# A decoder trunk whose MLP's second matrix goes in seven half-block products, woven with the first matrix of the next rows, and sums of its weights made by accumulating DMAs in DRAM

## The chip, the cores and the metric

The kernel runs on one core of a Trainium2 chip. The metric is device time in microseconds (us), the median of several executions. The engines are named as the profile names them: PE (TensorE, matrix products), DVE (VectorE), ACT (ScalarE), POOL (GpSimd) and SP (SyncE, which here only issues DMAs). PEld is PE's loading of the stationary operand, which runs beside the products.

## The reference, cut to what matters

One sequence of 1024 tokens, width 1024, goes through two layers. Layer 0 mixes tokens with attention and a gated delta rule, layer 1 with a recurrent block. After each mixer comes a layer norm, then an MLP of hidden width 4096, then a second norm.

```python
def sqrelu_mlp(x, w1, w2):
    h = jax.nn.relu(x @ w1)          # (1024, 1024) @ (1024, 4096)
    return (h * h) @ w2              # (1024, 4096) @ (4096, 1024)

def reference(x, ...):
    for layer in range(DEPTH):       # DEPTH = 2
        ...
        x = layer_norm(DN_ALPHA * x + mix, ln1_g[layer], ln1_b[layer])
        x = layer_norm(DN_ALPHA * x + sqrelu_mlp(x, mlp_w1[layer], mlp_w2[layer]),
                       ln2_g[layer], ln2_b[layer])
    return x
```

All is float32 with an output of (1, 1024, 1024).

## The kernel before

**Products.** Each float32 operand is split into a rounded part h and a residue l. A product is then three matmuls, h by h, h by l and l by h (`mm3`, line 359), added up in one PSUM bank. One matmul has 128 x 128 stationary elements and up to 512 moving columns. In the tables a "product" of PE is one such matmul.

**Weights.** `wblock` (line 339) loads a block of 128 x 1024 elements (512 KB) on SP's queue into one of three buffers `ws`, and splits it by halves: the rounded copy `wh` on ACT (every fifth half on DVE), the residue `wl` by turns on POOL and DVE. There are four half-block buffers for each of `wh` and `wl`, thus two blocks.

**Two streams.** The tokens go in two chunks of 512 rows, stream 0 and stream 1 (`stream`, line 1158). Stream 1 needs stream 0's states in the mixers, so it runs behind it. All of PE's work is put into one fixed order at build time. The driver loop (line 1190) asks the streams' generators for work: a `yield UNIT` ends a piece after which another stream may come next, a `yield BLOCK` means that a stream waits for buffers or for the other. The stream with the lowest `phase` (0 for mixers, 1 and 2 for the two MLPs) comes first; recurrent blocks (`light`) take turns with the other stream. Small mixer parts and norms are spawned as generators of their own and come in when a rough model of the engines (class `Clock`) says that their operands are there. The other engines' order is made by the tile framework's scheduler, with a simulated timeline.

**Buffers.** `gpool` has 14 granules of 128 x 2048 elements (`g`): an activation matrix with its residue (`ActT`) takes four, the residual rows `yg` of a stream two. Rings `t` (11), `s` (9) and `f` (4) hold tiles of 128 x 516. PSUM has four banks `mm` and four `mx`.

**MLP** (`mlp`, line 500). Eight passes e, each over 512 hidden columns. First matrix: four blocks by `proj_fm` (line 412), each 24 matmuls into one bank; ACT applies Relu and Square, POOL squares again in full precision, DVE makes the residue; the results (`s`) are hidden columns on partitions. Second matrix: for each half of the 1024 outputs, two blocks, 48 matmuls into four banks, which DVE then adds to y (128 x 512 each). In the last pass DVE also makes the norm's statistics (`bn_stats`). The last pass of stream 1 in layer 1 goes row block by row block, so that the final norm can start early.

**Norms** (`layernorm`, line 450). DVE makes the coefficients, ACT, DVE and POOL scale the eight halves, PE transposes them, ACT and DVE split the transposed rows into h and l. `mix_out` (line 1117) does a mixer's output projection (`out_proj`) and then such a norm; `mlp_ln` (line 1131) does an MLP and the norm behind it.

**Recurrent block** (`rec_block`, line 944). Four for each stream, each with four projection blocks of 24 matmuls, one block of gate weights (24 matmuls), and a chain of about 20 operations on ACT and DVE for each of its two columns, in tiles of ring `t`.

## Time and profile before

| | us |
|---|---|
| median of 3 runs | 2389.71 |
| lowest, highest | 2389.05, 2390.38 |
| span of the profiled execution | 2384.5 |
| PE busy | 2298.9 |
| DVE busy | 1345.1 |
| ACT busy | 912.7 |
| POOL busy | 843.0 |

The span goes from the first to the last instruction; the profile gives no total time of its own execution, and the median lies 5.2 us above the span. Busy times of different engines overlap. A busy time in a matmul's or vector operation's row includes its pipeline, so operations that follow one another start closer together than their mean durations say. All compute operations that the planner's wrappers issue have line 177 or, for PE, 204 and 207; the tiles' names tell them apart: `wh`, `wl`, `ws` are weights, `g` granules, `mm` and `mx` PSUM, `w` in a DMA an MLP matrix, `hout` and `rout` output projections, `rin` and `rg` recurrent weights.

### The profile page before, as it was taken

To read this page: it belongs to the slowest core of one execution; us is meant where nothing else is said; L and a number is where in the kernel's file an instruction comes from. 1 tells how busy PE (TensorE), PEld (TensorE's weight loads), DVE (VectorE), ACT (ScalarE), POOL (GpSimd) and SP (SyncE) were. 2 spreads that over 40 slices of the span, in tenths; PEclk is the share of its full clock that TensorE was granted. 3 is DMA by queue.
4 is the path that set the end of the run, shared out by engine and by line. 5 is a ranking of instruction groups with operands and counts; after the bars stand their busy time and mean duration, and the time that the engine had idled before them with its cause. 6 is when DMAs were issued, how large, how long until landed. Compare 5 with 4: busy or idle time off the path is not lost. (4 is left out here: it accounts for less than half of the span.)

```text
span 2384.5 us, 33354 instructions
## 1 busy us (share of the span) xinstructions
PE 2298.9 (96%) x12724; PEld 1841.9 (77%) x12724; DVE 1345.1 (56%) x2550; ACT 912.7 (38%) x1813; POOL 843.0 (35%) x706
## 2 busy tenths in 40 slices
PE   8889997999999999999999999999999999999997
PEld 7666775677777878778887788877887788778876
DVE  7697659565754463755664623565665543633345
ACT  5364424443333242454443322344554232322331
POOL 3342334232332243433443432343333333433341
PEclk9999998999999999999999999999999999999999
DMA  4121231122233222322333222232325222332231
GB/s 154 54 81 31 81 124 36 54 69 74 73 114 110 95 88 98 123 89 97 98 131 125 82 96 97 97 121 91 98 93 177 85 97 97 107 115 98 98 117 51
DMA packets 67487, 227.43 MB, mean 95 GB/s; under 512 B 7424, under 2 KB 7808, under 8 KB 67328
## 3 DMA queue, kind: packets, MB, share of 16 engines
q1 hardware_dynamic: 58832, 204.01, 25.9%
q10 hardware_dynamic: 8496, 21.30, 2.5%
q8 instruction: 100, 1.64, 0.3%
q14 instruction: 59, 0.48, 0.1%
HBM read 216.89 MB, written 8.39 MB: 94 GB/s over the span
## 5 line engine op out<-in xcount | busy, mean ns | idle before, releaser
L177 POOL TENSOR_TENSOR wl<-ws,wh 128x512 fp32r<-128x512 f32 (+1 forms) x372 | 497.6, 1338 | 1261.4 <-ACT wh L177 979.4
L204 PE MATMUL mm<-g,wh 128*128 128x512 f32 x2816 | 886.7, 396 | 0.5 <-DVE g L177 0.5
L177 ACT CAST wh<-ws 128x512 fp32r<-128x512 f32 (+1 forms) x595 | 365.5, 616 | 993.0 <-PE mm L204 910.1
L204 PE MATMUL mm<-wh,s 128*128 128x512 f32 x1984 | 648.2, 399 | 11.4 <-ACT s L177 5.7
L204 PEld LDWEIGHTS mm<-g,wh 128*128 128x128 f32 x2816 | 520.2, 189 | 107.2 <-issue 2.9
L204 PE MATMUL mm<-g,wl 128*128 128x512 f32 x1408 | 550.9, 391 | 5.4 <-POOL wl L177 5.4
L204 PEld LDWEIGHTS mm<-wh,s 128*128 128x128 f32 x1984 | 374.0, 189 | 102.6 <-ACT s L177 6.2
L204 PE MATMUL mm<-wl,s 128*128 128x512 f32 x992 | 391.9, 395 | 2.3 <-POOL wl L177 1.4
L177 DVE TENSOR_TENSOR wl<-ws,wh 128x512 fp32r<-128x512 f32 (+1 forms) x372 | 281.2, 756 | 188.8 <-ACT wh L177 184.4
L204 PEld LDWEIGHTS mm<-g,wl 128*128 128x128 f32 x1408 | 265.1, 188 | 64.0 <-POOL wl L177 7.1
L204 PE MATMUL mm<-wh,g 128*128 128x512 f32 (+1 forms) x768 | 235.2, 380 | 10.0 <-ACT wh L177 6.1
L177 DVE TENSOR_TENSOR s<-s,s 128x512 fp32r<-128x512 f32 x128 | 100.4, 784 | 242.9 <-POOL s L177 231.1
L204 PEld LDWEIGHTS mm<-wl,s 128*128 128x128 f32 x992 | 187.4, 189 | 43.3 <-POOL wl L177 1.8
L177 DVE TENSOR_TENSOR g<-g,mm 128x512 f32<-128x512 f32 x224 | 144.0, 680 | 130.7 <-PE mm L204 130.5
L204 PEld LDWEIGHTS mm<-wh,g 128*128 128x128 f32 x768 | 142.0, 190 | 38.7 <-ACT wh L177 6.1
L177 DVE CAST wh<-ws 128x512 fp32r<-128x512 f32 (+1 forms) x149 | 73.8, 495 | 172.6 <-PE mm L204 165.0
L177 POOL TENSOR_TENSOR s<-s 128x512 f32<-128x512 f32 x128 | 145.3, 1135 | 26.4 <-ACT s L177 26.4
L204 PE MATMUL mm<-wl,g 128*128 128x512 f32 (+1 forms) x384 | 143.7, 374 | 0.1
L177 ACT ACTIVATE s<-mm 128x512 f32<-128x512 f32 x128 | 75.9, 593 | 62.1 <-PE mm L204 61.9
L177 ACT ACTIVATE s<-s 128x512 fp32r<-128x512 f32 (+1 forms) x136 | 83.5, 614 | 19.0 <-DVE s L177 8.0
L204 PEld LDWEIGHTS mm<-wl,g 128*128 128x128 f32 x384 | 72.9, 190 | 11.9 <-DVE wl L177 0.4
L204 PE MATMUL mx<-g,wh 128*128 128x512 f32 x256 | 78.8, 389 | 0.0
(209 smaller groups left out, 2230.3 us busy)
## 6 DMA issues: line engine op xcount, KB each, us to landing
ws<-w SPq DMA_DIRECT2D x256, 512.0 KB, 3.3
ws<-hin_fm SPq DMA_DIRECT2D x32, 512.0 KB, 3.3
ws<-rin SPq DMA_DIRECT2D x32, 512.0 KB, 3.3
ws<-hout SPq DMA_DIRECT2D x16, 512.0 KB, 3.4
ws<-rout SPq DMA_DIRECT2D x16, 512.0 KB, 3.4
t<-ln ACTq DMA_DIRECT2D x28, 256.0 KB, 4.2
ws<-hin_q SPq DMA_DIRECT2D x8, 512.0 KB, 3.2
g<-x ACTq DMA_DIRECT2D x8, 512.0 KB, 5.0
```

The source lines that it names most:

```text
L177: r = f(*a, **k)
L204: return self._pe(self.pe.matmul(out, lhsT, rhs, start=start, stop=stop), out, [lhsT, rhs], c, start)
```

## The change

**Seven products.** Where it applies, a quarter j of the hidden width (1024 columns, two passes) is treated as a 2 x 2 block product: the hidden activations of 512 rows as two row halves (256 rows) by two column halves (512), the second matrix's quarter as two by two blocks of 512 x 512. In place of eight block products there are seven (`seven`), on combinations of the blocks. The combinations of activations are made by four DVE operations in place, 1024 elements wide. The combinations of weights `t1` to `t4` are sums that are ready in DRAM. Three accumulators of two banks each are begun; later products add on to a bank that has already been read (`kept`, banks `mm` and `mx`), and what stands there after each product is added to, or subtracted from, y.

**Sums of weights.** `w2_sums` is spawned in stream 0's first mixer. For each layer and quarter it copies four blocks of 1 MB from DRAM to DRAM on SP's queue and adds seven more by accumulating DMAs on POOL's queue, in rounds. `seven` waits in the build order until a quarter's sums are issued; on the chip the loads wait for their data.

**The MLP's order.** `first` makes the hidden values of one quarter and stores them unsplit, without POOL. `weave` then alternates one first-matrix block of the next quarter with two units of `seven` of this one. The straight passes stay where the condition fails: stream 0 until stream 1's output projection of the layer is through, at even e and with two granules free. In stream 1 of layer 1 pass 6 goes straight first, and the last pass (`ends`, `finish`) keeps its order by rows; its four hidden tiles are stored unsplit and split by `finish` after the last weave.

**Waits between the streams.** Stream 1's norm behind a mixer waits (`hold`) until stream 0's MLP has used its last first-matrix block (`m7`); stream 0's norm behind MLP 0 waits for the same of stream 1. Stream 1's recurrent block b waits for stream 0's block b, and uses ring `s` in place of `t`.

**Weights.** Three buffers of whole blocks in place of four of half blocks, split by one operation 1024 wide for each part; in `first` and `seven` the residue is always DVE's. The second matrix is stored by quarters and blocks.

```diff
-WB, HV, LG = 4, 5, 2
-RINGS = dict(t=11, s=9, f=4)
+WB, WS, HV, LG = 3, 3, 5, 2
+RINGS = dict(t=11, s=10, f=4)
...
+    def split(h, l, x, key):
+        wcount[0] += 1
+        (V.tensor_copy if wcount[0] % HV == 0 else S.copy)(h, x)
+        (G if key else V).tensor_tensor(l, x, h, ALU.subtract)
+    def wblock(src, n=1024, hl=None, pool=True):
+        st = clk.tile("ws", WS, wpool.tile([P, 1024], F32, tag="ws", name=nm("ws"), bufs=WS))[:, :n]
+        DS.dma_start(st if len(src.shape) == 2 else st.rearrange("p (q c) -> p q c", q=2), src)
+        if hl is None:
+            hl = [clk.tile(t, WB, wpool.tile([P, 1024], F32R, tag=t, name=nm(t), bufs=WB))[:, :n] for t in ("wh", "wl")]
+        h, l = hl
+        split(h, l, st, pool and wcount[0] % LG)
...
-    def proj_fm(src, x, bank=None):
-        wh, wl = wblock(src)
+    def proj_fm(src, x, bank=None, pool=True):
+        wh, wl = wblock(src, pool=pool)
...
+    SUMS = dict(t1=("b11", "b12"), t3=("b12", "b22"), t2=("b11", "b12", "b22"), t4=("b11", "b12", "b22", "b21"))
+    QUARTER = dict(b11=0, b12=1, b22=2, b21=3)
+    tsum = [[{k: dpool.tile([2 * P, D], F32, name=f"{k}_{i}_{j}", tag=f"{k}_{i}_{j}") for k in SUMS} for j in range(4)]
+            for i in range(2)]
+    def w2_quarter(layer, j, q):
+        return tsum[layer][j][q] if q in SUMS else I[f"w2_{layer}"][j * 4 + QUARTER[q]]
+    summed = set()
+    kept = [0]
+    def w2_sums():
+        rows = lambda x: x.rearrange("(a b) c -> a (b c)", b=2)
+        for layer, j in ((i, j) for i in range(2) for j in range(4)):
+            for k, (first, *_) in SUMS.items():
+                DS.dma_start(rows(tsum[layer][j][k]), rows(w2_quarter(layer, j, first)))
+            for i in range(1, 4):
+                t = clk.now + 8.0
+                yield lambda: t
+                for k, v in SUMS.items():
+                    if i < len(v):
+                        DG.dma_start(rows(tsum[layer][j][k]), rows(w2_quarter(layer, j, v[i])), accum_op=ALU.add, max_dma_last_dim=2048)
+            summed.add((layer, j))
+            t = clk.now + 8.0
+            yield lambda: t
...
+    def mlp(layer, c, yT, yg, ls, res=None):
+        w1 = I[f"w1_{layer}"]
+        seen = set()
+        def accumulate(ps, n, half, sign, done):
+            y = ytile(yg, n)[:, half * 512:(half + 1) * 512]
+            op = ALU.add if sign > 0 else ALU.subtract
+            if (n, half) not in seen:
+                seen.add((n, half))
+                V.scalar_tensor_tensor(y, y, ALPHA, ps, ALU.mult, op)
+            else:
+                V.tensor_tensor(y, y, ps, op)
+            if done:
+                V.bn_stats(ls[:, n, 6 * half:6 * half + 6], y)
+        either = lambda n: next((r for r in "st" if rings[r] >= n), None)
+        left = [32]
+        def used():
+            left[0] -= 1
+            if left[0] == 0:
+                yT.free()
+                st[c]["m7"] = layer
+        def straight(e, done):
+            j, i = divmod(e, 2)
+            yield from wait(lambda: either(8))
+            ring = either(8)
+            own = [(ts(ring, F32R), ts(ring, F32R)) for _ in range(4)]
             for f in range(4):
+                h, l = own[f]
                 ps = yield from proj_fm(w1[e * 4 + f], yT)
-                h, l, r = ts("s", F32R), ts("s", F32R), ts("s")
+                used()
+                r = clk.tile("r", 2, wpool.tile([P, 512], F32, tag="r", name=nm("r"), bufs=2))
                 S.activation(r, ps, AF.Relu)
                 S.activation(h, r, AF.Square)
                 G.tensor_tensor(r, r, r, ALU.mult)
                 V.tensor_tensor(l, r, h, ALU.subtract)
-                free("s", r)
-                sh.append(h)
-                sl.append(l)
-                if e == 7 and f == 3:
-                    yT.free()
                 yield UNIT
-            if e == 7 and res is not None:
-                for n in range(NT):
-                    a, b = n * P, (n + 1) * P
-                    for half in range(2):
-                        ps = mm_ps()
-                        for f in range(4):
-                            wh, wl = wb[half * 2 + f // 2]
-                            mm3(ps, sh[f][:, a:b], sl[f][:, a:b], wh[f % 2], wl[f % 2], f == 0, f == 3)
-                            yield
-                        y = ytile(yg, n)[:, half * 512:(half + 1) * 512]
-                        V.tensor_tensor(y, y, ps, ALU.add)
-                        V.bn_stats(ls[:, n, 6 * half:6 * half + 6], y)
-                    res["n"] = n + 1
-                    if n == 0:
-                        res["start"]()
-                    yield UNIT
-                free("g", *own)
-                free("s", *sh, *sl)
-                return
...
+        def hidden(f, z):
+            ps = yield from proj_fm(w1[f], yT, mm_ps, False)
+            used()
+            S.activation(z, ps, AF.Relu)
+            S.activation(z, z, AF.Square)
+            yield UNIT
+        def seven(j, g, done):
+            yield from wait(lambda: (layer, j) in summed)
+            A = {f"a{r + 1}{q + 1}": v4(g[q])[:, :, r * 256:(r + 1) * 256] for q in range(2) for r in range(2)}
+            bank = {}
+            for i, (a, b, acc, out, sign, last) in enumerate((
+                    ("a12", "b21", "R", (0, 0), 1, False), ("a11", "b11", "X", (0, 0), 1, True),
+                    ("a21", "t1", "R", (1, 1), 1, False), ("a21", "t2", "X", (0, 1), -1, False),
+                    ("a12", "b22", "R", (0, 1), 1, True), ("a21", "t3", "X", (1, 1), -1, True),
+                    ("a22", "t4", "X", (1, 0), 1, True))):
+                if i == 2:
+                    V.tensor_tensor(A["a21"], A["a21"], A["a22"], ALU.subtract)
+                elif i == 3:
+                    V.tensor_tensor(A["a21"], A["a21"], A["a11"], ALU.subtract)
+                elif i == 4:
+                    V.tensor_tensor(A["a12"], A["a12"], A["a21"], ALU.add)
+                elif i == 5:
+                    V.scalar_tensor_tensor(A["a21"], A["a21"], -1.0, A["a22"], ALU.mult, ALU.subtract)
+                start = i < 3
+                if start:
+                    bank[acc] = [(mm_ps if acc == "X" else mx_ps)() for _ in range(2)]
+                    kept[0] += 2 * (acc == "X")
+                for p in range(2):
+                    yield from wait(lambda: either(2))
+                    ring = either(2)
+                    ah, al = ts(ring, F32R), ts(ring, F32R)
+                    ah2, al2 = (z.rearrange("p (k t) -> p k t", k=2) for z in (ah, al))
+                    x = A[a][:, 2 * p:2 * p + 2]
+                    S.copy(ah2, x)
+                    V.tensor_tensor(al2, x, ah2, ALU.subtract)
+                    wh, wl = wblock(w2_quarter(layer, j, b)[p * P:(p + 1) * P], pool=False)
+                    for k in range(2):
+                        for t in range(2):
+                            mm3(bank[acc][t], ah2[:, k, t * P:(t + 1) * P], al2[:, k, t * P:(t + 1) * P], wh[k], wl[k],
+                                start and p + k == 0, p + k == 2, not start)
+                            if p + k == 2:
+                                accumulate(bank[acc][t], 2 * out[0] + t, out[1], sign, done and last)
+                            if k + t < 2:
+                                yield
+                    free(ring, ah, al)
+                    if i == 6 and p == 1:
+                        free("g", *g)
+                        kept[0] -= 2
+                    yield UNIT
+        def first(j):
+            yield from need("g", 2)
+            g = [gran() for _ in range(2)]
+            for f in range(8):
+                yield from hidden(j * 8 + f, v4(g[f // 4])[:, f % 4, :])
+            hids[j] = g
+        def weave(a, b, every):
+            left = [(a, 1), (b, every)] if a is not None else [(b, every)]
+            while left:
+                stuck = True
+                for gen, k in list(left):
+                    for _ in range(k):
+                        r = next(gen, "end")
+                        if r is BLOCK:
+                            break
+                        stuck = False
+                        while r is not UNIT and r != "end":
+                            yield r
+                            r = next(gen, "end")
+                        if r == "end":
+                            left.remove((gen, k))
+                            break
+                        yield UNIT
+                if stuck:
+                    yield BLOCK
+        hids = {}
+        e = 0
+        if res is not None:
+            yield from straight(6, False)
+        while e < 8 and not ((c == 1 or sts[1].get("op", -1) >= layer) and rings["g"] >= 2 and e % 2 == 0):
+            yield from straight(e, e == 7)
+            e += 1
+        if e < 8:
+            n = 3 if res is not None else 4
+            yield from first(e // 2)
+            for j in range(e // 2, n):
+                nxt = first(j + 1) if j + 1 < n else ends() if res is not None else None
+                yield from weave(nxt, seven(j, hids.pop(j), j == 3), 2)
+        if res is not None:
+            yield from finish()
...
-    def mix_out(w, oT, resid, which, r, s, t):
+    def mix_out(w, oT, resid, which, r, s, t, hold):
...
+        s["ln0"]["op"] = which // 2
         s["yT"] = ActT()
+        yield from wait(hold)
         yield from need("g", 4)
...
     def mlp_ln(layer, c, s, r, last):
...
             if not last:
+                if c == 0:
+                    yield from wait(lambda: "m7" in sts[1])
                 yield from need("g", 4)
+                s["x"].claim()
...
     def stream(c):
...
-        if c == 0:
-            yield from wait(lambda: "ln1" in st[1])
-        else:
-            yield from wait(lambda: "rec" in st[0])
...
         for b in range(4):
+            yield from wait(lambda: c == 0 or sts[0].get("rb", 0) > b)
...
-            yield from rec_block(c, b, s["x"], hT, s)
+            yield from rec_block(c, b, s["x"], hT, s, "ts"[c])
+            st[c]["rb"] = b + 1
...
```

More of the change, by code (lines that the diff above doesn't have):

```diff
@@ L544, in mlp @@
             for half in range(2):
+                yield from wait(lambda: kept[0] == 0)
                 ps = [mm_ps() for _ in range(NT)]
                 for p in range(2):
-                    wh, wl = wblock(w2[(e * 2 + half) * 2 + p])
-                    for j in range(2):
-                        f = 2 * p + j
+                    wh, wl = wblock(w2_quarter(layer, j, f"b{i + 1}{half + 1}")[p * P:(p + 1) * P])
+                    for k in range(2):
+                        h, l = own[2 * p + k]
@@ L561, in mlp @@
-                            if f < 3 or n < NT - 1:
+                            mm3(ps[n], h[:, a:b], l[:, a:b], wh[k], wl[k], p + k == 0, p + k == 2)
+                            if p + k == 2:
+                                accumulate(ps[n], n, half, 1, done)
+                            if p + k < 2 or n < NT - 1:
                                 yield
                 if half == 1:
-                    free("s", *sh, *sl)
+                    free(ring, *(z for hl in own for z in hl))
                 yield UNIT
+        def hidden(f, z):
[4 more added lines that the diff above has]
+            yield UNIT
@@ L570, in out_proj @@
         for half in range(2):
+            yield from wait(lambda: kept[0] == 0)
             ps = yield from proj_tm([w[half * 4 + i] for i in range(4)], oT, 512)
@@ L972, in rec_block @@
             i = 2 * b + j
[L973 to L974 removed]
+            yield from need(ring, 1)
+            g2 = ts(ring)
             ps = yield from proj_fm(I["rin"][4 * b + 2 + j], x, mx_ps)
@@ L1001, in rec_block @@
             if j == 1:
-                free("t", *xch, *xcl)
-                reg[1] = [ts("t") for _ in range(4)]
+                free(ring, *xch, *xcl)
+                reg[1] = [ts(ring) for _ in range(4)]
             r, a, iv, w = reg[j]
```

133 lines of the change are left out of this document (66 added, 67 removed).

## The prediction

> **What bounds the kernel now.** I read the page's busy shares first, then the busy times in stretches of 60 us, then TensorE's timeline in the MLP, then the other engines' groups.
>
> ```profile
> span 2384.5 us, 33354 instructions
> PE 2298.9 (96%) x12724; PEld 1841.9 (77%) x12724; DVE 1345.1 (56%) x2550; ACT 912.7 (38%) x1813; POOL 843.0 (35%) x706
> ```
>
> PE is busy in 96% of the span, so 85.6 us are without a product. Where these lie, and what the others do there, stands in the table of stretches (columns: stretch, length, then PE, PEld, DVE, ACT, POOL busy, clock, DMA share, GB/s):
>
> ```profile
> 300.00:360.00 60.00, 59.20 (x264) 47.49 (x263) 33.84 (x67) 16.32 (x40) 19.15 (x16) 1.00 0.38 126
> 360.00:420.00 60.00, 44.91 (x394) 33.24 (x394) 55.85 (x135) 29.85 (x72) 28.05 (x21) 0.86 0.10 33
> 960.00:1020.00 60.00, 57.80 (x268) 47.01 (x267) 46.17 (x72) 25.01 (x43) 27.11 (x22) 1.00 0.36 123
> 1020.00:1080.00 60.00, 57.90 (x255) 47.37 (x254) 32.55 (x42) 32.20 (x53) 24.00 (x23) 1.00 0.27 88
> 1080.00:1140.00 60.00, 60.00 (x265) 49.28 (x264) 31.22 (x44) 29.75 (x49) 19.83 (x19) 1.00 0.29 97
> 1140.00:1200.00 60.00, 60.00 (x262) 48.91 (x261) 34.69 (x45) 30.66 (x49) 22.24 (x20) 1.00 0.30 97
> 1200.00:1260.00 60.00, 60.00 (x263) 49.11 (x262) 37.21 (x45) 27.11 (x46) 25.06 (x23) 1.00 0.37 132
> 1320.00:1380.00 60.00, 56.87 (x257) 46.05 (x256) 35.86 (x57) 25.78 (x43) 27.41 (x20) 0.97 0.24 79
> 1860.00:1920.00 60.00, 56.79 (x256) 45.80 (x255) 43.06 (x72) 20.70 (x34) 23.47 (x16) 0.97 0.28 92
> 1920.00:1980.00 60.00, 60.00 (x263) 49.14 (x262) 19.15 (x32) 16.33 (x27) 19.22 (x16) 1.00 0.28 91
> ```
>
> In the MLP (last row) PE never stops and DVE is busy a third of the time. Two streams of 512 rows cover each other: while one is in a norm or in recurrent blocks (1020 to 1260), the other's MLP fills PE. The 25% gap at 360 to 420 is a stage where DVE itself is full. So the bound is the number of products. What one costs is the distance between starts:
>
> ```profile
> 1003.07 0.61 PE L204 MATMUL mm<-g,wh 128*128 128x512 f32 x2
> ...
> 1008.51 0.39 PE L204 MATMUL mm<-wh,s 128*128 128x512 f32 x1
> ...
> 1019.62 0.61 PE L204 MATMUL mm<-g,wh 128*128 128x512 f32 x2
> ```
>
> The first two rows hold 24 products of the first matrix between them, 5.44/24 = 0.2267 us each; the next 48 are of the second matrix, 11.11/48 = 0.2315 us.
>
> **What goes.** A quarter of the second matrix (1024 hidden rows, two e) takes 2 x 96 = 192 products straight. In seven half-block products it takes 7 x 24 = 168. That is 24 x 0.2315 = 5.56 us less for each quarter done so. There are 16 quarters, but not all qualify: stream 0 may begin only when stream 1 is through the layer's output projection, at an even e. The weight loads, in order, tell when that is:
>
> ```profile
> 350.97 120.62 SPq L177 DMA_DIRECT2D ws<-w  x11
> 518.59 44.13 SPq L177 DMA_DIRECT2D ws<-w  x7
> 577.04 0.33 SPq L177 DMA_DIRECT2D ws<-w  x1
> 608.22 39.42 SPq L177 DMA_DIRECT2D ws<-w  x7
> 661.85 93.06 SPq L177 DMA_DIRECT2D ws<-w  x14
> 761.25 40.03 SPq L177 DMA_DIRECT2D ws<-hout x8
> ```
>
> Before stream 1's projection, stream 0 has loaded 40 blocks, eight for an e: five of its eight e are straight, the sixth must follow, and one quarter is left for seven products. Stream 1 in layer 0 does all four, stream 0 in layer 1 four (three if it starts early), stream 1 in layer 1 three, as its last quarter stays straight. I take 12 (bounds 9 to 13): **-66.7 us** (-50 to -72).
>
> **What the seven products put on DVE.** For each quarter: 14 weight residues 1024 wide instead of eight blocks shared with POOL, 14 residues of the activations, 14 additions to y, four combinations 1024 wide, some casts, in the last quarter eight statistics.
>
> ```profile
> 863.64 1.87 DVE L177 TENSOR_TENSOR g<-g,mm 128x512 f32<-128x512 f32 x3
> ...
> 829.71 0.70 DVE L177 SCALAR_TENSOR_TENSOR g<-g,lnw,t 128x512 f32<-128x512 f32 x1
> ...
> 837.82 11.10 DVE L177 TENSOR_TENSOR g<-g,t 128x512 f32<-128x512 f32 x9 [0.22 <-ACT g L177]
> ...
> 859.71 0.68 DVE L177 TENSOR_TENSOR g<-mx,g 128x512 fp32r<-128x512 f32 x1
> ```
>
> Three 512-wide operations take 1.87 us, so 0.6 each when they follow one another. No row has a 1024-wide one; it lies between 0.6 and 1.2, and I take 1.2, twice the row, since the width is what is streamed. A quarter then costs DVE 16.8 + 8.4 + 8.4 + 4.8 + 2 = 40.4 us, 45.2 with statistics. Woven with the next eight first-matrix blocks (8 x 1.2 = 9.6) it is 50 us beside 168 x 0.2315 + 192 x 0.2267 = 82.4 us of PE: covered, as DVE's work was. ACT gets 14 copies more and is far from full. Nothing is charged there; if DVE's order failed, each combination that PE waited for would cost some 3 us, four in a quarter.
>
> Not covered is the last quarter of a stream, which has no next first matrix: 38.9 us of PE against 45.2 of DVE. And just then the other stream's norm starts, since the new waits hold it until the last first-matrix block is used (it needs the granules). The norm above takes 31 us from 829.7 to 860.4; its own DVE part is 11.1 for the nine, 1.3 for two more, eight residues (4.8) and about 5 for the coefficients, 22 us. DVE has 67 us, PE 38.9 and some 7 for transposes. Before, such a norm cost PE 1 to 3 us, as the rows at 1320 and 1860 show. The difference is 21 us; DVE works some 5 us ahead in three weight buffers, and the last 3 us (additions, statistics) hold nobody up: 13 us. This happens three times: stream 0 in layer 0, stream 1 in layer 0, stream 0 in layer 1. At the second, stream 0's recurrent blocks take turns with the rest, and I count 6. **+32 us** (0 to 63). What queues behind the held norm is only its own stream, which had work for PE just the same; what then waits is PE.
>
> **Recurrent blocks.** Stream 0's norm is held until stream 1's first matrix is through, so its recurrent blocks lose the MLP as filler and run beside stream 1's. The four rows from 1020 to 1260 hold 135.7 us of DVE and 119.7 of ACT for four blocks. A block is five weight blocks, 27.2 us of PE; four are 109, and the other 131 us are MLP at the density of the row at 1920 (DVE 42, ACT 36). That leaves 23 us of DVE and 21 of ACT for a block, below 27.2. So neither becomes the bound, but the slack is small. Bounds: nothing, or the quarter of PE that the row at 360 loses beside a full DVE (54 of 218 us). I take **+8 us**, nearer the rows where DVE is not full.
>
> **Sums of weights.** Per quarter of a layer four copies of 1 MB on SP's queue and seven accumulations of 1 MB on POOL's, in rounds 8 us apart in the planner's time, eight sets from about 60 us on. Each accumulation waits on POOL for the one before it on the same sum, and POOL's conv additions and half of the weight residues queue behind it. No row shows one. The nearest:
>
> ```profile
> q1 hardware_dynamic: 58832, 204.01, 25.9%
> ...
> ws<-w SPq DMA_DIRECT2D x256, 512.0 KB, 3.3
> ```
>
> 204 MB in 25.9% of 2384.5 us are 330 GB/s, so 1 MB takes 3.2 us of all engines (and a load of half of it lands in 3.3); an accumulation reads twice, so 3.2 to 6.4. A set is 35 to 58 us against the planner's 32, so POOL could stand for 3 to 26 us a set, 24 to 208 in all. POOL is busy 19 of 60 us in the row at 300, and weight buffers are three blocks deep (16 us of PE), so most of a wait is hidden; below nothing it can't go, since it is work added. The bounds are 0 and 208; I take **+10 us**. SP's loads stand behind four copies, 13 us, within the same 16. The sums themselves are wanted from about 850 us on, long after.
>
> The Trainium skill speaks against this step: its page "DMA: Bandwidth & Descriptors", section "Two DMAs through the same engine are not ordered", says that only the completion semaphore orders two transfers, so the issuing engine must wait. No run here shows it yet. Its section "Anatomy of one DMA — SWDGE (gpsimd) path" gives 2.0 us and bytes at 436 GB/s, an estimate of 4.4 us for 1 MB; by that the term would be much the same.
>
> **Small terms.** Norm stalls: the stretches from 960 on lose about 20 us to norms; some of these norms move under the woven stages or are the ones charged above, **-9** (0 to -20). Weight waits: three buffers of whole blocks for two,
>
> ```profile
> L204 PE MATMUL mm<-g,wl 128*128 128x512 f32 x1408 | 550.9, 391 | 5.4 <-POOL wl L177 5.4
> ```
>
> and POOL out of the MLP's weights, **-5** (0 to -10). At the end four splits stand between the last weave and the last products, **+2**.
>
> Sum: -66.7 + 32 + 8 + 10 - 9 - 5 + 2 = -28.7, a span of 2355.8 us. The runs shown have a median of 2389.7, 5.2 above the profiled span; so **2361 us**.
>
> **The rivals.**
> 1. *DVE takes PE's place* (slower). Place: the three unwoven quarters and the recurrent stage. If the norm and the quarter share DVE with no head start, 3 x 21 = 63, and if the recurrent chains lose half of the upper bound, 27, the sum is -66.7 + 63 + 27 + 10 - 9 + 2 = +26: 2416. It decides when these losses pass 60 us. For it: 67 against 46 us, and the row at 360. Against: the recurrent rows at 1080 to 1260, with no PE gap.
> 2. *POOL stands in the sums* (slower). If a wait comes through to PE for 10 us a set, 80 in place of 10: 2431. For it: accumulations in POOL's queue, early, where PE already has gaps. Against: POOL's idle two thirds.
> 3. *Almost the whole gain*: the two streams' work hides the unwoven quarters, 6 us in all, recurrent blocks nothing: -66.7 + 6 + 4 - 9 - 5 + 2 = -69: 2321.
> 4. *It does not do what it says*: the conditions (granules, the other stream's projection, even e) leave only some six quarters: -33 + 32 + 8 + 10 - 9 = +8: 2398, or about no change.
>
> **How the numbers follow.** Forecast 0.45 (2340 to 2382), rival 1 0.23, rival 2 0.10, rival 3 0.12, rival 4 0.10. About 0.2%, 5 us, is what a measurement of this kernel can tell from no change. Faster: forecast and rival 3 whole, a little of rival 4: 0.58. Same: 0.08, from rivals 4 and 1. Slower: 0.34. The range 2318 to 2430 leaves out the far ends of rivals 1 and 2, some 0.16; the likeliest case alone has 2340 to 2382.
>
> **What would show it.** Second-matrix products in the after trace: 12 x 24 = 288 fewer than before. In the woven stretches PE at 60 of 60 with DVE at 35 to 40. Three stretches with PE down by some 13 us while DVE is full, each at a norm. POOL's accumulations between 60 and 400 us, with PE there not below the rows of before by more than 10 us in all. It is wrong if PE waits for DVE inside the weave, if the recurrent stage shows gaps, or if POOL's DMA waits appear as the releaser of weight residues.

## The result, and the profile after

| | before | after |
|---|---|---|
| median of 4 executions, us | 2389.38 | 2852.72 |
| lowest, highest | 2388.11, 2390.38 | 2848.64, 2855.02 |
| span of the profiled execution | 2384.5 | 2851.4 |

The ratio is 1.194 (95% interval 1.192 to 1.196): 463 us slower, where 2361 was predicted, in a range of 2318 to 2430. The page of after, busy times first:

```profile
span 2851.4 us, 32067 instructions
PE 2257.5 (79%) x12436; PEld 1811.8 (64%) x12436; DVE 1559.3 (55%) x2560; ACT 1018.8 (36%) x1742; POOL 537.8 (19%) x383
```

PE has 288 products and 41.4 us of busy time less, so the saving is there, and the span is 467 us longer all the same. Section 2 of the same page (40 slices of 71 us) shows where:

```profile
PE   3011111378988899999999999969899999999998
PEclk7555555689999999999999999989999999999999
```

For eight slices PE is at three tenths or less, at 0.5 to 0.7 of its clock. The stretches of after (PE, PEld, DVE, ACT, POOL busy, clock, DMA share, GB/s):

```profile
60.00:120.00 60.00, 0.00 (x0) 0.00 (x0) 0.00 (x0) 0.00 (x0) 1.03 (x1) 0.50 1.03 325
120.00:180.00 60.00, 15.01 (x50) 11.03 (x50) 5.95 (x9) 6.11 (x10) 11.45 (x13) 0.61 0.76 155
...
360.00:420.00 60.00, 5.45 (x15) 3.88 (x16) 2.71 (x4) 0.63 (x1) 10.98 (x11) 0.51 0.72 124
...
540.00:600.00 60.00, 32.14 (x564) 22.33 (x550) 16.58 (x41) 4.34 (x8) 15.53 (x13) 0.72 0.75 139
600.00:660.00 60.00, 52.66 (x323) 40.85 (x323) 50.77 (x131) 36.82 (x106) 23.83 (x22) 0.94 0.28 88
...
1380.00:1440.00 60.00, 56.88 (x265) 46.38 (x264) 42.24 (x52) 28.41 (x41) 0.00 (x0) 1.00 0.38 126
...
1560.00:1620.00 60.00, 60.00 (x266) 49.71 (x265) 38.40 (x45) 26.70 (x36) 0.00 (x0) 1.00 0.42 139
...
1860.00:1920.00 60.00, 37.52 (x173) 30.81 (x172) 41.54 (x61) 32.23 (x48) 21.18 (x14) 0.83 0.33 114
...
2040.00:2100.00 60.00, 47.51 (x203) 38.70 (x204) 51.68 (x54) 36.68 (x55) 27.65 (x16) 0.86 0.16 55
```

Two things are to be seen. In the first 600 us, no compute engine works much: none of them is the bound, they all wait, while the DMA engines (second column from the end) are at 0.7 or more. From 600 us on the kernel runs as planned, with a full PE in the woven MLP (1560) and some gaps beside recurrent blocks (1860, 2040). SP's timeline says how the first stretch begins (start, length, queue, operation, out<-in, count):

```profile
13.00 6.68 SPq L178 DMA_DIRECT2D t<-w  x4
...
23.56 36.65 SPq L178 DMA_DIRECT2D t<-w  x12
62.77 0.33 SPq L178 DMA_DIRECT2D ws<-hin_fm  x1
65.80 38.75 SPq L178 DMA_DIRECT2D t<-w  x12
138.14 12.16 SPq L178 DMA_DIRECT2D ws<-hin_fm  x2
...
590.31 3.08 SPq L178 DMA_DIRECT2D ws<-xT  x2
```

All 32 copies of the sums (`t<-w`) are issued before 105 us, those of layer 1, wanted over 1000 us later, among them. Twelve take 38.75 us, 3.2 each, as the prediction had it; but from 23 to 105 us SP issues a single block of mixer weights. Stream 1's first rows (`ws<-xT`) are fetched at 590.31; before, at 94.16. That difference of 496 us is about the whole loss. What comes after the copies is POOL's own queue, in its timeline (in brackets the idle time before, and what ended it):

```profile
212.86 1.02 POOL L178 DMA_DIRECT2D t<-w  x1 [7.42 <-issue]
221.59 1.03 POOL L178 DMA_DIRECT2D t<-w  x1 [7.72 <-issue]
230.21 1.01 POOL L178 DMA_DIRECT2D t<-w  x1 [7.59 <-issue]
...
274.57 2.74 POOL L178 TENSOR_TENSOR wl<-ws,wh 128x1024 fp32r<-128x1024 f32 x1
283.48 1.02 POOL L178 DMA_DIRECT2D t<-w  x1 [6.17 <-issue]
```

Each accumulation takes 1 us to issue, and POOL stands 7.6 us before the next, with no semaphore that the profile could name ("issue"). From 204 to 274 us nine accumulations go out with nothing between them; only behind them comes the one weight residue (`wl`) at 274.57. The groups and the DMA rows of the page:

```profile
q0 software_dynamic: 29568, 58.72, 12.4%
...
L206 PE MATMUL mm<-g,wl 128*128 128x512 f32 x1408 | 555.6, 395 | 187.1 <-POOL wl L178 185.8
...
L178 DVE SCALAR_TENSOR_TENSOR f<-f,sm,f 128x512 f32<-128x512 f32 x48 | 42.1, 876 | 299.2 <-POOL f L178 298.8
...
L178 POOL DMA_DIRECT2D t<-w x56 | 57.7, 1030 | 488.5 <-issue 437.3
...
t<-w POOLq DMA_DIRECT2D x56, 1024.0 KB, 8.3
```

An accumulation lands 8.3 us after its issue, and the next is issued 8.6 us after it: one at a time. 12.4% of 2851.4 us over 56 are 6.3 us of all 16 DMA engines each. POOL is busy with all this for 57.7 us only, while its queue stands for 488.5; the busy share doesn't show it. Who waits for it is in the table of waits of 100 to 600 us (who, for whom: total, times, longest):

```profile
POOL t L178 <- issue: 401.5, 53, 29.1
DVE f L178 <- POOL f L178: 288.8, 6, 112.6
...
PE mm L206 <- POOL wl L178: 284.1, 5, 105.6
...
PE mm L206 <- ACT wh L178: 98.5, 4, 46.3
...
PE mm L206 <- DVE wh L178: 86.5, 2, 74.9
```

Five waits of PE for a weight residue, 57 us each in the mean: not one 8 us wait after another, but POOL's one residue behind a row of accumulations that the order put before it. PE waits another 185 us for rounded weights of ACT and DVE (98.5 and 86.5). Whether POOL is behind these too is told by the chain that ended last, by engine, in section 4 of the page:

```profile
PE 64%; issue 15%; DVE 11%; DMA 4%; POOL 3%; ACT 2%; SPq 0%; ACTq 0%; DVEq 0%; POOLq 0%
```

The 15% are 428 us, nearly all of it POOL's standing: from 107 to 580 us the chain's long pieces are waits of 4 to 9 us in POOL's queue, one behind the other (the first one is of 27 us). Before that, from 11 to 107 us, they are transfers of the sums.

### The profile page after: what moved, and what is told of

Same layout as the page of the kernel before. It is cut to its first block, busy times and chain, and to the rows that moved or that the text cites. A ratio compares the mean times of both kernels' runs of the same rounds, so it can differ in the third digit from the quotient of the medians.

```text
span 2851.4 us, 32067 instructions
## 1 busy us (share of the span) xinstructions
PE 2257.5 (79%) x12436; PEld 1811.8 (64%) x12436; DVE 1559.3 (55%) x2560; ACT 1018.8 (36%) x1742; POOL 537.8 (19%) x383
## 3 DMA queue, kind: packets, MB, share of 16 engines
q0 software_dynamic: 29568, 58.72, 12.4%
## 4 chain that ended last, share of the span: by engine, by line
PE 64%; issue 15%; DVE 11%; DMA 4%; POOL 3%; ACT 2%; SPq 0%; ACTq 0%; DVEq 0%; POOLq 0%
PE mm L206 49%; PE mx L206 14%; DVE g L178 4%; DMA t<-w 3%; POOL t L178 2%; PE mx L210 1%; DVE f L178 1%; DVE s L178 1%; DVE hsc L178 1%; DVE wl L178 1%; DVE t L178 1%; POOL wl L178 1%; ACT wh L178 1%; ACT g L178 1%; DVE lnw L178 1%
## 5 line engine op out<-in xcount | busy, mean ns | idle before, releaser
L178 DVE TENSOR_TENSOR wl<-ws,wh 128x1024 fp32r<-128x1024 f32 (+1 forms) x349 | 433.0, 1242 | 336.5 <-ACT wh L178 333.3
L178 ACT CAST wh<-ws 128x1024 fp32r<-128x1024 f32 (+1 forms) x356 | 370.7, 1042 | 673.9 <-PE mm L206 613.7
L178 POOL TENSOR_TENSOR wl<-ws,wh 128x1024 fp32r<-128x1024 f32 (+1 forms) x95 | 239.8, 2524 | 994.2 <-ACT wh L178 830.9
L206 PE MATMUL mm<-wh,s 128*128 128x512 f32 x1152 | 377.7, 395 | 10.3 <-DVE g L178 3.5
L206 PEld LDWEIGHTS mm<-wh,s 128*128 128x128 f32 x1152 | 217.1, 189 | 58.8 <-ACT s L178 4.1
L206 PE MATMUL mm<-wl,s 128*128 128x512 f32 x576 | 225.2, 391 | 0.0
L206 PE MATMUL mx<-wh,s 128*128 128x512 f32 x576 | 187.5, 393 | 1.2 <-DVE s L178 1.2
L178 POOL DMA_DIRECT2D t<-w x56 | 57.7, 1030 | 488.5 <-issue 437.3
L178 DVE TENSOR_TENSOR s<-g,s 128x512 fp32r<-128x512 f32 x172 | 118.8, 706 | 50.0 <-ACT s L178 49.9
L206 PEld LDWEIGHTS mx<-wh,s 128*128 128x128 f32 x576 | 108.6, 189 | 24.3 <-DVE s L178 2.0
L206 PE MATMUL mx<-wl,s 128*128 128x512 f32 x288 | 112.3, 390 | 0.0
```

What stands on the lines that cost most here:

```text
L178: r = f(*a, **k)
L206: ins = self.pe.matmul(out, lhsT, rhs, start=start, stop=stop, skip_group_check=fresh)
```

## The experiments

Seven questions, one after the other. A time without an interval comes from a single execution.

**What does the rest of the change cost without the sums?**

```diff
-                DS.dma_start(rows(tsum[layer][j][k]), rows(w2_quarter(layer, j, first)))
+                planned(rows(tsum[layer][j][k]), rows(w2_quarter(layer, j, first)), False)
...
-                        DG.dma_start(rows(tsum[layer][j][k]), rows(w2_quarter(layer, j, v[i])), accum_op=ALU.add, max_dma_last_dim=2048)
+                        planned(rows(tsum[layer][j][k]), rows(w2_quarter(layer, j, v[i])), True)
```

`planned` enters the transfer in the planner's model and issues nothing, and `seven` loads a plain block in place of a sum; PE's fixed order stays.

> The change with the sums of weights left out: no copies, no accumulations; each product that took a sum takes the plain block that the sum begins with, so the output differs, while the order of TensorE's work and its 12 quarters in seven products stay. Theory A (the whole loss is the sums, all of it in the first 600 us, where stream 1's first transfer starts 496 us later than before): 2340 to 2375 us, and that transfer again near 100 us. Theory B (the reorganisation loses too, the gaps at 1860 and 2040 us of the changed kernel being typical): 2400 us or more.

Measured: 2357.88 us, ratio 0.9875 (0.9858 to 0.9891), as theory A has it; stream 1's first rows are fetched at 81.80 us. So the sums cost 494.8 us, and the rest of the change brings 30.5 us.

**Copies or accumulations?** The copies stay, the accumulations are left out (only the second of the two edits above).

> The 32 copies from DRAM to DRAM stay, the 56 accumulations are left out, so the sums are incomplete and the output differs. Theory A (the copies, issued ahead of the weights on the same queue, hold the weights back; 32 MB at 330 GB/s is 100 us): 80 to 110 us over the kernel without sums. Theory B (the accumulations in POOL's queue are nearly the whole loss): within 30 us of the kernel without sums.

Measured: 2439.12 us, in theory A's range. The copies cost 81 us, the accumulations on top of them the other 414. In the stretches of this kernel PE stops for most of one, with the DMA engines full, and then goes on:

```profile
60.00:120.00 60.00, 12.14 (x50) 9.09 (x50) 9.12 (x29) 6.96 (x24) 5.04 (x5) 0.59 0.97 326
120.00:180.00 60.00, 54.68 (x698) 41.66 (x701) 35.56 (x77) 17.84 (x40) 21.28 (x16) 0.91 0.24 80
```

In the first 120 us PE works 49 us here and 107 without sums. These 58 us fall in the time of the copies; the rest of the 81 comes later and was not traced.

**Are the sums slow by themselves, whatever the MLP's order?** The kernel before with `w2_sums` added; nobody reads the sums.

```diff
+            spawn(w2_sums(), 60.0)
...
-    nc = _bacc.Bacc("TRN2", target_bir_lowering=False, num_devices=1)
+    nc = _bacc.Bacc("TRN2", target_bir_lowering=False, num_devices=1, dynamic_dma_scratch_size=2048)
```

> The kernel before, with the change's 32 copies and 56 accumulations added and nobody reading the sums; products, buffers and order of the streams as before. Theory A (the loss is in the sums alone, whatever reads them): 2389 + 495 = 2840 to 2920 us. Theory B (the loss needs the change's other parts, such as the deeper or fewer weight buffers): less than 2750.

Measured: 2892.01 us, 504 over the kernel before on the same chip, as theory A has it. The weave, the holds and the seven products are not needed for the loss.

**One at a time: larger descriptors.** A transfer is cut into pieces, each told to the DMA engines by a descriptor; `max_dma_last_dim` bounds a piece's size. Pieces of 8192 bytes in place of 2048:

```diff
-                        DG.dma_start(rows(tsum[layer][j][k]), rows(w2_quarter(layer, j, v[i])), accum_op=ALU.add, max_dma_last_dim=2048)
+                        DG.dma_start(rows(tsum[layer][j][k]), rows(w2_quarter(layer, j, v[i])), accum_op=ALU.add, max_dma_last_dim=8192)
```

> As the change, but each accumulation's descriptors are 8 KB instead of 2 KB; every engine's order is the same but for these. Theory A (POOL stands because its descriptor memory has room for one accumulation at a time): several are in flight, POOL's 437 us of waiting for issue go, the distance between accumulations falls from 8.6 to about 6.3 us, the DMA engines' own time, and the total falls by 100 us or more to about 2700. Theory B (the wait is the transfer's own duration, whatever the descriptors): within 30 us of 2852.

Measured: 2643.9 us, 209 faster than the change; theory A had some 2700, with 6.3 us between accumulations. Its page's DMA rows, and POOL's timeline:

```profile
q0 software_dynamic: 8064, 58.72, 11.0%
...
t<-w POOLq DMA_DIRECT2D x56, 1024.0 KB, 36.2
```

```profile
243.38 0.83 POOL L178 DMA_DIRECT2D t<-w  x1 [4.10 <-issue]
248.29 0.82 POOL L178 DMA_DIRECT2D t<-w  x1 [4.07 <-issue]
253.17 0.81 POOL L178 DMA_DIRECT2D t<-w  x1 [4.06 <-issue]
```

Packets fall from 29568 to 8064, that is from 33 to 9 on each of 16 engines for an accumulation. They are issued 4.9 us apart and land after 36.2: seven are under way where there was one, and the DMA engines, at 0.72 to 0.76 in the change from 120 us on, are at 1.01 or more from 60 to 360 us. So in the change POOL stood because the next transfer could not be queued; now it stands beside DMA engines that are full. That room for descriptors is what was short (the change sets `dynamic_dma_scratch_size` to 2048) is argued from the pieces' size alone; another size of that room wasn't tried. A rival is that POOL stands because making the descriptors of 33 packets for each engine takes that long; the spread kernel below, with the same small pieces, speaks against it.

**Bunched: the framework's order or the planner's times.** First, copies and accumulations keep their place in program order (with 2048 and with 8192 bytes):

```diff
-                DS.dma_start(rows(tsum[layer][j][k]), rows(w2_quarter(layer, j, first)))
+                tc.keep_in_program_order(DS.dma_start(rows(tsum[layer][j][k]), rows(w2_quarter(layer, j, first))))
...
-                        DG.dma_start(rows(tsum[layer][j][k]), rows(w2_quarter(layer, j, v[i])), accum_op=ALU.add, max_dma_last_dim=2048)
+                        tc.keep_in_program_order(DG.dma_start(rows(tsum[layer][j][k]), rows(w2_quarter(layer, j, v[i])), accum_op=ALU.add, max_dma_last_dim=2048))
```

> As the change, but the copies stay behind whatever was traced before them on SP's queue, and the accumulations on POOL's, so the framework's scheduler can't move them to the front; TensorE's order is the same. Theory A (what costs is that they all come first): the copies no longer stand at 8 to 105 us, and the total falls by about 100 us for them and more for the accumulations, to 2450 to 2650. Theory B (56 accumulations of 8.6 us are 480 us of POOL's time in front of the convolutions wherever they stand in the first mixers): 2750 or more.

> Kept in order as in the earlier run, in the change's own rounds of 8 us, with descriptors of 8 KB. The two single steps gave 2658 (order) and 2644 (descriptors). Theory A (a set takes 4 x 3.2 + 7 x 4.9 = 47 us of all DMA engines against 32 us in the plan, so about 15 us a set, 120 us in all, are lost besides the weights' delay): 2450 to 2540. Theory B (the two remedies add up and hide the sums): 2400 or less.

Measured: 2657.9 and 2460.69 us; the first is between the two theories, 8 us over A's range, the second within A's. In the first, the copies now go out in fours from 30 to 536 us, and stream 1's first rows are fetched at 82.23, so the copies no longer hold them up; what that alone is worth was not measured. Yet PE is at 20 to 53 of 60 there in every stretch up to 720 us: the accumulations still come in rounds of four, two and one, the first five of them in a row from 74 to 112 us, and stand in front of POOL's residues. Order and size together take away 392 of the 495 us.

Then the same sums, one transfer at a time, spread in the planner's time: copies 5 us apart, accumulations 16 (the old entries become `planned`, so PE's order stays).

```diff
+    def real_sums():
...
+                        tc.keep_in_program_order(nc.gpsimd.dma_start(rows(tsum[layer][j][k]), rows(w2_quarter(layer, j, v[i])), accum_op=ALU.add, max_dma_last_dim=2048))
+                        t = clk.now + 16.0
+                        yield lambda: t
```

> All sums are made, from 60 us on as in the change, but spread: copies 5 us and accumulations 16 us apart in the planner's time, each kept behind what was traced before it on its queue; descriptors 2 KB as in the change; TensorE's plan is that of the change. Theory A (what costs is that POOL and the DMA engines have more to do with the sums than the stretch allows, not that the sums exist): with one accumulation of 8.6 us each 16 us or more, POOL rarely stands, and the time is within 40 us of the kernel without sums (2358), so 2360 to 2400. Theory B (each accumulation costs the path its own time wherever it stands): 56 x 8.6 minus what idle stretches hide, 2550 or more.

> As the spread kernel, with descriptors of 8 KB. Theory A (POOL's descriptor memory and the engines' time of 8.6 against 4.9 us for one accumulation are what is left): 2355 to 2375 us, faster than the kernel before by 0.6 to 1.4%, and 5 to 30 us under the spread kernel with 2 KB. Theory B (spread out, an accumulation is hidden either way): within 5 us of the spread kernel with 2 KB.

Measured: 2385.39 with 2048 bytes, and 2388.02 with 8192, ratio 1.0003 (0.9994 to 1.0013). The first is as its theory A has it; for the second theory A, 2355 to 2375, failed, and B holds. Nearly all is gone, but 30 us over the kernel without sums are left, and a larger descriptor no longer helps. The kernel with 2048 bytes also shows what one accumulation costs POOL when no other is close:

```profile
92.89 1.07 POOL L542 DMA_DIRECT2D t<-w  x1
93.56 1.29 POOL L178 TENSOR_TENSOR g<-kraw,angles 128x128 f32<-128x128 f32 x2
```

POOL's next operation starts 0.67 us behind it. So an accumulation with small pieces doesn't hold POOL for 7.6 us by itself; POOL stands only when another transfer follows too soon. Whether descriptors are still being made meanwhile the trace doesn't tell.

Up to 720 us PE works 667 us in the kernel with 8192 bytes and 669 without sums: hardly any loss. It comes later:

```profile
840.00:900.00 60.00, 54.44 (x232) 42.58 (x231) 35.20 (x43) 22.94 (x33) 4.94 (x6) 1.00 0.97 269
...
1020.00:1080.00 60.00, 54.38 (x212) 42.98 (x211) 33.95 (x40) 24.84 (x35) 3.31 (x4) 0.89 0.76 214
...
1140.00:1200.00 60.00, 56.11 (x240) 45.77 (x239) 27.44 (x32) 19.50 (x26) 4.92 (x6) 0.97 0.89 263
```

These are woven stretches, where PE was at 60 without sums, with 266 or 267 products in each; DMA is at 0.76 to 0.97 against 0.42 to 0.46 there. From 720 to 1320 us this kernel does 139 products less than the one without sums, which at 60/266 us each are 31 us, the whole difference. Keeping the order keeps no distance: once POOL has little else to do (4.94 of 60 us), its transfers follow one another as fast as they can, beside MLP weights.

**A distance that the chip keeps.** One 1 MB transfer, copy or accumulation, every 16 us of the planner's time, and each also waits for PE's latest product in the order.

```diff
+                        tc.keep_in_program_order(d)
+                        tc.add_manual_dep(d.ins, clk.last.ins.name, SYNC, reason="pace")
+                        t = clk.now + 16.0
```

> All sums made, one transfer of 1 MB (a copy or an accumulation, descriptors of 8 KB) every 16 us of the planner's time, each also waiting on TensorE's latest product so that the pace holds on the chip. The spread kernel with 8 KB lost its 30 us from 840 us on, where the DMA share stood at 0.8 to 0.97. Theory A (there transfers bunch and the weights' loads come late): with the pace held, 2355 to 2375 us, faster than the kernel before by 0.6 to 1.4%. Theory B (any transfer beside the woven stage costs, bunched or not): 2380 or more.

Measured: 2364.24 us (2360.36 to 2366.6), ratio 0.9892 (0.9876 to 0.9909), as theory A has it. All 32 copies and 56 accumulations are made, 6.4 us over the kernel without any. This kernel makes the whole change and is 1.1% faster than the kernel before. In the same three stretches:

```profile
840.00:900.00 60.00, 60.00 (x267) 49.69 (x266) 39.98 (x46) 27.68 (x39) 1.61 (x2) 1.00 0.66 203
...
1020.00:1080.00 60.00, 60.00 (x267) 49.68 (x266) 39.07 (x45) 27.03 (x36) 2.44 (x3) 1.00 0.72 205
...
1140.00:1200.00 60.00, 60.00 (x266) 49.67 (x266) 37.85 (x44) 25.22 (x34) 2.46 (x3) 1.00 0.69 197
```

PE waits for weights from 720 to 1320 us for 0.8 us in all. This kernel differs from the one before it in two points, the wait for PE and the copies' distance (16 for 5); which of the two did more wasn't separated.

**Why only 30 us, where 24 products less for each of 12 quarters are 67?** Every quarter straight, no sums, all else as in the change:

```diff
-        if res is not None:
-            yield from straight(6, False)
...
+        while e < (7 if res is not None else 8):
...
-        if e < 8:
-            n = 3 if res is not None else 4
-            yield from first(e // 2)
...
+            yield from ends()
```

> The kernel without sums, with every quarter done straight: no seven products, no combinations, the products of the kernel before, but the change's weight buffers, waits between the streams and order of recurrent blocks; the output is the reference's. Theory A (the reorganisation costs 30 us or more, chiefly the gaps in the recurrent stage, and the seven products bring nearly their full 66.7): 2405 to 2430. Theory B (the reorganisation is nearly free and the seven products lose half of their gain to DVE): 2380 to 2400.

Measured: 2432.47 us, ratio 1.0182 (1.0167 to 1.0197), 2 us over theory A's range. The seven products are worth 74.6 us (2432.47 to 2357.88), and the order around them costs 44. Which part of it? The three holds that keep a norm until the other stream's first matrix is through are taken out of this kernel:

```diff
-                if c == 0:
-                    yield from wait(lambda: "m7" in sts[1])
...
-                           "s" if c == 0 else "t", s, st[c]["t"], lambda: c == 0 or "m7" in sts[0])
+                           "s" if c == 0 else "t", s, st[c]["t"], lambda: True)
...
-                           lambda: c == 0 or sts[0].get("m7") == 1)
+                           lambda: True)
```

> As the straight kernel without sums, but the three waits by which a norm is held until the other stream's first matrix is through are taken out, so a stream's norm and recurrent blocks may again run under the other stream's MLP. Theory (the holds cost what the reorganisation costs: 43 us beside before): 2385 to 2400 us, PE at 58 or more of 60 in the stretches of the recurrent blocks. Rival (the loss comes from the other parts: recurrent blocks one behind the other, whole-block weight buffers, ring s): 2420 to 2435 us, with PE at 43 to 57 of 60 in some stretch of the recurrent blocks as it was.

and, in the paced kernel, the wait of stream 1's recurrent block b for stream 0's is taken out:

```diff
-            yield from wait(lambda: c == 0 or sts[0].get("rb", 0) > b)
```

> As the paced kernel with all sums, but stream 1's recurrent block b no longer waits for stream 0's block b. Theory (the holds make the loss, as both streams' mixers and a norm have to be done with no MLP beside them): within 5 us of 2364. Rival (the order of the blocks makes it): some 20 us faster, 2340 to 2350, with no gaps of PE in the stretches from 1320 to 1740.

Measured: 2401.14 us, ratio 1.0056 (1.0039 to 1.0072), and 2361.42, ratio 0.9889 (0.9875 to 0.9904). The first misses its theory's range by 1 us; the second is as its theory has it. The holds cost 31 of the 44 us; the order of the blocks costs nothing that can be told (3 us). A stretch of the straight kernel with the holds, and two of the one without:

```profile
1320.00:1380.00 60.00, 43.73 (x196) 36.23 (x195) 40.48 (x65) 21.54 (x31) 21.36 (x15) 0.86 0.33 114
```

```profile
1320.00:1380.00 60.00, 60.00 (x270) 49.42 (x269) 32.63 (x53) 15.51 (x19) 17.93 (x9) 1.00 0.25 81
1380.00:1440.00 60.00, 58.58 (x271) 48.36 (x269) 26.57 (x34) 18.66 (x27) 25.29 (x14) 1.00 0.32 101
```

Not every stretch is so full without the holds (51.75 of 60 at 960, 53.63 at 1500). From 960 to 1740 us, where the recurrent blocks and most of the norms around them lie, PE is idle for 50 us with the holds and 27 without. One wait leads PE's waits from 1260 to 1740 us with the holds, 17.7 us in all in the straight kernel and this in the kernel without sums, with seven products:

```profile
PE mx L210 <- DVE g L178: 23.9, 3, 22.0
```

Without the holds it is 2.1 us, and in the kernel before 1.0. A single wait of 22 us: PE's next entry in its fixed order is a transpose of rows of stream 1's norm behind its first MLP. DVE makes that norm's statistics at 1363 us of the kernel without sums and scales the first rows at 1380; PE goes on at 1390. Stream 0, which was held, is still in its recurrent blocks and has no MLP to put beside it. In the kernel with seven products the holds are there to keep granules free for the hidden values, and dropping them there was not tried on the chip. What remains of the 44 us, some 13, was not traced further.

## Why the prediction was wrong

The sum of the chip's own steps, from the medians above: +13 for the reordering without holds (44 less 31), +31 for the holds, -75 for the products, +81 for the copies, +414 for the accumulations.

- **Sums of weights, +10 (0 to 208): measured +495.** This is the step that failed, and by itself it turns the sign. The prediction let "a set" take 35 to 58 us against the planner's 32, let POOL stand for the difference, and hid most of that behind three weight buffers. Three things in it were wrong. *When:* it took the planner's 8 us rounds for the chip's order, but the copies depend on nothing, and the framework put all 32 ahead of the mixers' weights (+81 with copies alone). Its sentence of four copies, 13 us, "within the same 16" had the right price for one set and missed that eight sets come at once. *How much:* the row of a plain load gave 3.2 to 6.4 us for an accumulation; its engine time is 6.3, within that, but with one under way POOL can issue one in 8.6 us. 56 x 8.6 are 482 us, more than the upper bound of 208, because that bound counted only what exceeds the planner's 32 us. *What is hidden:* POOL's idle two thirds was no cover. POOL's queue went in order, so that a residue of 2.5 us behind five accumulations of 8.6 us comes 43 us late, and the one at 274.57 us came 70 us behind the first of nine; the prediction's three buffers hold 16 us of PE.
- **Rival 2** named the mechanism (POOL stands in the sums, 0.10) but priced it at 10 us a set, 80 in all, and gave as its ground against it just that idle share.
- **The claim that would have shown it**: PE not over 10 us below before from 60 to 400 us: from 60 to 420 us PE works 42 us, where it was 322.

**What orders two transfers.** The rule of the section "Two DMAs through the same engine are not ordered" of the Trainium skill's page "DMA: Bandwidth & Descriptors" is that the issuing engine waits for completion between dependent transfers. The spread kernel with 8 KB pieces does so, and POOL waits 371.7 us for `t<-w` transfers there:

```profile
POOL t L542 <- DMA t<-w: 371.7, 19, 111.6
```

No run leaves the wait out, so the rule itself is not tested. In the change itself nearly all of the wait is another, with no semaphore in the profile. The estimate of 4.4 us for 1 MB by the section "Anatomy of one DMA — SWDGE (gpsimd) path" of the same page of the Trainium skill was too low for an accumulation: it lands after 8.3 us with 2 KB pieces in the change, and after 8.9 with 8 KB pieces in the paced kernel. Only the distance of 4.9 us, with seven under way, comes near.

**All other terms, -38.7: measured -30.5.** The mechanism held, with its terms off in both directions.

- *Twelve quarters, -66.7:* exactly 12 x 24 = 288 products are gone, and between the two kernels that differ in this they were worth 74.6 us.
- *Woven stretches with PE at 60 and DVE at 35 to 40:* so in after from 1500 to 1740 (the row at 1560: 60.00 and 38.40).
- *Unwoven quarters beside a norm, +32 (13, 6, 13), less 9 for norms that are covered now:* the stretches of after from 1380 to 1500, 1740 to 1860 and 2460 to 2580 lose 4, 5 and 8 us, 17 in all, against 23 of the two terms. PE does slow down at the three norms, but by less than DVE's 67 us beside PE's 46 let expect; why less wasn't tested.
- *Recurrent blocks, +8 (0 to 54):* the stretches from 1320 to 1740 without sums lose 40 us, and taking out the holds wins 31 in the straight kernel. That the held stream loses its filler was the prediction's own reason; its size was read from DVE's mean of 23 us a block beside 27 of PE, which says nothing of one 22 us wait for a norm's chain in PE's fixed order. That norm is stream 1's own, right behind its unwoven quarter: the sum charged the other stream's norm beside that quarter (6 us) and had no term for this one. "The recurrent stage shows gaps" was among the signs named for a wrong forecast.
- *The 5.2 us from span to median:* too much by some 3 us. The runs of after and of every experiment lie 1.7 to 1.9 us above their own span; by that the profiled execution of before took some 2386 us, and the 5.2 sets a median against the span of a faster execution.

## What to carry to other kernels

Work that "runs beside" on an idle engine is free only if nothing urgent stands behind it in that engine's queue: multiply the price of one by how many can stand in a row in front of the next urgent instruction, not by the engine's idle share. A transfer with no input that it waits for goes as early as a scheduler lets it, so bulk transfers need a dependency that ties them to the work beside which they are meant to run: the same 88 transfers of 1 MB cost 495 us bunched, 30 us in order and spread, and 6 us when each also waits for PE and the copies are spread as far as the accumulations. And where a new order removes the filler beside a chain, price the chain's longest single wait, not the mean load of its engines.

## What the runs showed of the hardware

- An accumulating 1 MB transfer in DRAM takes 6.3 us of all DMA engines in 2 KB pieces and 5.2 to 5.7 in 8 KB pieces (bunched, and paced), against 3.2 for a plain copy of the size.
- In these kernels, with 2048 of scratch for descriptors, how many of POOL's transfers are under way hangs on the pieces' size: one of 33 packets for each engine (8.6 us apart, landing after 8.3), seven of 9 packets (4.9 apart, landing after 36.2). While the next can't be queued POOL stands, with no semaphore that the profile could name; a transfer with 2 KB pieces and no other close behind costs POOL 1 us.
- With PE idle its granted clock stood at 0.50 (60 to 120 us of after, no product at all).
